# An encoder trunk on one core: recurrence outputs one segment later, weight scales inside the next projection, weight squares and casts in halves

## The chip, the cores and the metric

The kernel runs on one core of one Trainium2 chip. TensorE (PE) multiplies matrices, VectorE (DVE) and ScalarE (ACT) do elementwise work, GpSimd (POOL) does some more of it, and SyncE (SP) issues the DMAs. The metric is the device time of one execution in microseconds; lower is better. Time before: 2451.22 us, the median of 3 runs (2450.67 to 2451.57).

## The reference, cut to what matters

One residual layer of a bidirectional encoder on an input of 2048 positions by 1024 channels. One combined projection of the normalized input makes ten blocks of 1024 columns. Five of them feed a gated linear recurrence with 8 heads and a 128 x 128 state per head, once forward and once backward; three feed a spatial gating branch; two are merge gates. The rest of the layer (two branch projections, one output projection, norms) lies behind what is changed here.

```python
h = _rmsnorm(x, norm_w[layer])
proj = jnp.einsum('bsd,de->bse', h, w_in[layer])
(q_raw, ffwd_raw, fbwd_raw, i_raw, ga_raw, u_raw, v_raw, gb_raw, ma_raw, mb_raw) = jnp.split(proj, split_points, axis=-1)
...
"""S_t = diag(f_t) S_{t-1} + k_t v_t^T ; o_t = S_t^T q_t, chunkwise."""
...
q = heads(jax.nn.silu(q_raw)) * (HGRN_KDIM ** -0.5)
v = heads(i_raw)
k_f, g_f = _hgrn2_forget(ffwd_raw, lb_fwd)
k_b, g_b = _hgrn2_forget(fbwd_raw, lb_bwd)
o_fwd = _gla_chunked(q, heads(k_f), v, heads(g_f))
o_bwd = flip(_gla_chunked(flip(q), flip(heads(k_b)), flip(v), flip(heads(g_b))))
o = (o_fwd + o_bwd).transpose(0, 2, 1, 3)
o = _rmsnorm(o, gnorm_w)
```

## The kernel before

**Number format.** A projection is made of three fp16 matmuls, since both sides are split into a high and a low fp16 part: `mm3` (L207) runs over 8 blocks of the contraction and for each multiplies high by high, high by low and low by high, 24 matmuls in one PSUM bank. The input `xT` is split once. A weight *unit* is 256 columns of `w_in`: `halves` (L171) loads it in fp32 (`wraw`), squares it on ACT to get the sum of squares (L180), casts that sum on GpSimd (`wsb`, L184), sums it over the partitions with a one-column matmul into `misc` (L189), makes a power-of-two scale of it with four small operations on DVE (`pow2`), and then makes the high part on ACT (L199) and the low part on DVE (L200). The first `yield` stands after the square, so `load` (L163) is everything before the `misc` matmul and calling its result is the rest. `unit` (L147) hands out the next unit and keeps up to two more under way. The pool of the units has five buffers of 8 KB a partition, and each unit takes two, so a unit's load waits until an older unit is used up.

**Loops.** `phase1` (L274) goes over four pairs of heads. For each pair it projects the values `i` of all four segments of 512 positions (`v_seg`, 96 matmuls of 256 columns a segment), then for each of the two heads the forward direction over segments 0 to 3 and the backward one over segments 3 to 0. Forward, a segment's query projection (`q_seg`, 24 matmuls of 512 columns) comes before its forget-gate projection (24 more); backward it is the gate projection alone. The first head's queries are projected earlier, beside the input's normalization.

**One segment.** `gla_operands` (L397) projects the gate, takes two sigmoids of it on ACT (`fz` L406, `kk` L408) and makes the decayed operands on DVE with two scans: `ff` (L437, the query side), `kt` (the key side), the decays `e8`, and on GpSimd `q0` (L453), the queries against the state at the segment's begin. `gla_products` (L460) then does, for four blocks of 128 positions: the scores `sc` (L477, L480) and the transposed keys `pk` (L479) on TensorE; the masks on DVE (L485, L498, and backward the sums L507); the copy `ks` of the keys on ACT (L500); the state products `pu` (L513); and then block by block the outputs `po` from scores (L517, backward only, where `at` holds both directions' scores) and from the state before the block (L519), and the state update `st` on DVE (L525). The outputs are evicted on ACT (`of`, L532) or added to the forward ones on DVE (`ob`, L534), squared on ACT (L538), normalized on GpSimd (L539 to L541) and stored in `o_d` (L339).

The work is software-pipelined by one segment: `finish(late)` (L331) runs the products of the segment before, after the operands of the present one. All engines' instructions are put in order when the program is built, by priorities and the builder's own estimate of when things are ready; `high_priority(URGENT)` raises masks, key copies and state updates. Each engine then runs its own list strictly in order and waits on semaphores.

After the recurrence the value projection of the gating branch begins (`wv`, two units of 512 columns each, `values` L761). Six of its tiles are made before a flag is read (L1261) and all engines pass a branch.

Of the kernel before, what the change touches and what calls it, by code (L numbers as in the profile page):

```python
# [27 lines left out]
P = 128  # L28
# [23 lines left out]
class Trunk:  # L52
# [85 lines left out]
    def plan(self):  # L138
# [6 lines left out]
        self.todo, self.made = todo, []  # L145
# [25 lines left out]
    def halves(self, w, c0, width):  # L171
# [3 lines left out]
        for i in range(width):  # L175
# [3 lines left out]
            ss = sm.tile([P, 1], F32, name="wss")  # L179
            nc.scalar.activation(out=(wt[:, 1] if wt is not None else got[0][1][:, 0]), in_=raw, func=AF.Square,  # L180
                                 accum_out=ss)

            sb = sm.tile([P, 1], BF16, name="wsb")
# [4 lines left out]
        for i, (_, _, sb) in enumerate(got):  # L188
            nc.tensor.matmul(pb, self.ones16, sb, start=(i == 0), stop=(i == width - 1))  # L189
# [6 lines left out]
        for raw, wt, _ in got:  # L196
            if wt is None:
                wt = self.wu.tile([P, 2, K, N], F16, name="wsplit")
            nc.scalar.activation(out=wt[:, 0], in_=raw, func=AF.Copy, scale=s)  # L199
# [7 lines left out]
    def mm3(self, ps, lh, ll, rh, rl):  # L207

        nc = self.nc
        for k in range(KT):  # L210
            nc.tensor.matmul(ps, lh(k), rh(k), start=(k == 0), stop=False)  # L211
            nc.tensor.matmul(ps, lh(k), rl(k), start=False, stop=False)  # L212
            nc.tensor.matmul(ps, ll(k), rh(k), start=False, stop=(k == KT - 1))  # L213

# [59 lines left out]
    def phase1(self):  # L274
        nc, tc = self.nc, self.tc
        with ExitStack() as es:
# [7 lines left out]
            self.gs = E(tc.tile_pool(name="g_s", bufs=4, **R))  # L284
# [5 lines left out]
            with tc.tile_pool(name="xp", bufs=3) as self.xp:  # L290
# [8 lines left out]
                for b in range(NSEG):  # L299
# [11 lines left out]
                    qs[b] = self.q_seg(0, 0, b, *wq)  # L311
            self.decays()
# [16 lines left out]
            state, of, late = None, [None] * NSEG, None  # L329

            def finish(seg):  # L331
                nonlocal state
                h, hh, d, s, ops, v = seg
                state, o = self.gla_products(hh, d, *ops, v, state if s != (0 if d == 0 else NSEG - 1) else None,
                                             of[s] if d else None)
                if d == 0:
                    of[s] = o
                else:
                    nc.sync.dma_start(out=self.o_d[4 * s:4 * s + 4, h].rearrange("c p v -> p c v"), in_=o)  # L339

            for hp in range(H // 2):
# [9 lines left out]
                wf = self.unit(self.w_in, C_FF + U * hp)  # L351
                wb = self.unit(self.w_in, C_FB + U * hp)
                for hh in range(2):
                    h = 2 * hp + hh
                    for d in range(2):
                        for s in (range(NSEG) if d == 0 else range(NSEG - 1, -1, -1)):
                            if h and d == 0:
                                qs[s] = self.q_seg(h, hh, s, *wq)
                            ops = self.gla_operands(h, hh, d, s, *(wb if d else wf), qs[s])
# [1074 lines left out]
```

## Time and profile before

| | |
|---|---|
| median of 3 runs | 2451.22 us (2450.67 to 2451.57) |
| the profiled execution's own time | 2447.7 us |
| its span, first to last instruction | 2446.0 us |
| mean granted TensorE clock | 0.995 |
| matmuls in it | 12860 |
| recurrence segments | 8 heads x 2 directions x 4 = 64 |
| their stretch of the span | about 110 to 1016 us |

How to read the rows that follow. A row of the timeline gives the start, the duration, the engine, the line of the kernel, the operation, output and inputs, and how many like it were merged; in brackets stands how long the engine was idle before and who ended that. An fp32 matmul is recorded as two passes, so that "x8" are four of them. A row of the groups by line ends with "busy us, mean ns of one | idle before it and who ended it". A row of the stretches gives the stretch, its length, and busy time (with the number of instructions) of PE, PEld, DVE, ACT and POOL, then the granted clock and the DMA's share and rate. A row of the waits gives the engine, tile and line that waited, for whom, the total, the number and the longest. DMA rows give size and the time from issue to landing.

### The profile page before, as it was taken

The numbers are of one execution on the slowest core, as the hardware profiler recorded it, in microseconds if no ns is written. First come the engines' busy times: TensorE is split into PE (matmuls) and PEld (weight loads), VectorE is DVE, ScalarE is ACT, GpSimd is POOL, SyncE is SP. The second block draws the span as 40 slices with busy tenths as digits, with TensorE's granted clock in tenths as the row PEclk, the third lists the DMA queues.
The fourth block names the chain that finished last, engine by engine and source line by source line (L and its number), as shares of the span: only waits on it lengthen the run. The fifth ranks groups of instructions, "written<-read, shape, count | busy, mean of one in ns | idle before, by whom it ended". The sixth has DMA issues, their size and how long they took to land. (4 is left out here: it accounts for less than half of the span.)

```text
span 2446.0 us, 33707 instructions
## 1 busy us (share of the span) xinstructions
PE 2355.1 (96%) x12860; PEld 1293.8 (53%) x12860; DVE 1523.8 (62%) x3014; ACT 1021.4 (42%) x1811; POOL 320.1 (13%) x523
## 2 busy tenths in 40 slices
PE   7999999999999999999999999999999999999998
PEld 5665766576658565544445544444444444444443
DVE  6686646654765476767555555667765564676754
ACT  6533333333333333423354545666655542244432
POOL 2121202120212021261000000000000000000011
PEclk9999999999999999999999999999999999999999
DMA  5100110011001000202322322577664773777733
GB/s 184 67 10 26 36 35 14 22 36 35 14 23 35 18 14 23 68 29 86 122 94 78 96 90 82 189 267 271 234 232 141 250 267 129 271 245 276 249 122 120
DMA packets 169483, 281.22 MB, mean 115 GB/s; under 512 B 10976, under 2 KB 105184, under 8 KB 162144
## 3 DMA queue, kind: packets, MB, share of 16 engines
q1 hardware_dynamic: 169312, 278.98, 33.6%
q8 instruction: 102, 1.67, 0.3%
q14 instruction: 69, 0.57, 0.1%
HBM read 174.08 MB, written 104.86 MB: 114 GB/s over the span
## 5 line engine op out<-in xcount | busy, mean ns | idle before, releaser
L728 PEld LDWEIGHTS <-seven 128*128 128x128 f16 x5376 | 524.6, 98 | 633.5 <-issue 23.5
L728 PE MATMUL bank<-seven 128*128 128x512 f16 x2016 | 438.2, 379 | 8.5 <-DVE zs L742 7.4
L728 PE MATMUL bank<-xT,seven 128*128 128x512 f16 x1920 | 428.8, 380 | 1.7 <-ACT zs L695 1.6
L728 PE MATMUL bank<-xs,seven 128*128 128x512 f16 x1440 | 322.1, 380 | 0.0
L211 PE MATMUL pin<-xT,wsplit 128*128 128x512 f16 x768 | 291.0, 379 | 0.2 <-ACT xT L256 0.2
L213 PE MATMUL pin<-xT,wsplit 128*128 128x512 f16 x768 | 291.1, 379 | 0.0
L212 PE MATMUL pin<-xT,wsplit 128*128 128x512 f16 x768 | 291.0, 379 | 0.0
L211 PE MATMUL pin<-wsplit,xT 128*128 128x256 f16 (+1 forms) x768 | 239.9, 312 | 11.2 <-ACTq L795 4.7
L213 PE MATMUL pin<-wsplit,xT 128*128 128x256 f16 (+1 forms) x768 | 239.8, 312 | 2.2 <-DVE xT L257 2.1
L212 PE MATMUL pin<-wsplit,xT 128*128 128x256 f16 (+1 forms) x768 | 239.6, 312 | 1.3 <-DVE wsplit L200 1.2
L742 DVE SCALAR_TENSOR_TENSOR zs<-bank,us,zs 128x512 f32<-128x512 f32 x120 | 89.0, 747 | 74.2 <-PE bank L728 71.7
L749 ACT ACTIVATE zs<-zs 128x512 f32<-128x512 f32 x120 | 75.4, 628 | 139.6 <-DVE zs L742 139.3
L742 DVE SCALAR_TENSOR_TENSOR zs<-bank,su,zs 128x512 f32<-128x512 f32 x72 | 53.9, 749 | 108.9 <-PE bank L728 85.4
L410 DVE TENSOR_SCALAR fz<-fz,fb,fa 128x512 f32<-128x512 f32 x64 | 35.7, 558 | 133.1 <-ACT fz L406 133.1
L213 PEld LDWEIGHTS <-wsplit 128*128 128x128 f16 x768 | 75.2, 98 | 79.5 <-issue 3.0
L212 PEld LDWEIGHTS <-wsplit 128*128 128x128 f16 x768 | 75.2, 98 | 71.7 <-issue 1.4
L211 PEld LDWEIGHTS <-wsplit 128*128 128x128 f16 x768 | 77.0, 100 | 67.2
L623 DVE TENSOR_TENSOR tmp<-raw 128x512 f32<-128x512 f32 x64 | 43.9, 690 | 106.6 <-ACT tmp L609 98.7
L519 PE MATMUL po<-st,q 128*128 128x128 f32 x480 | 99.4, 290 | 10.4 <-DVE st L525 7.1
L695 ACT ACTIVATE zs<-bank,us 128x512 f32<-128x512 f32 x120 | 80.6, 678 | 58.7 <-PE bank L728 56.1
L212 PEld LDWEIGHTS <-xT 128*128 128x128 f16 x768 | 76.0, 99 | 44.9 <-issue 10.0
L519 PEld LDWEIGHTS po<-st,q 128*128 128x128 f32 x480 | 72.9, 189 | 48.1 <-DVE st L525 38.6
(202 smaller groups left out, 3610.1 us busy)
## 6 DMA issues: line engine op xcount, KB each, us to landing
kept<-seven SPq DMA_DIRECT2D x16, 1792.0 KB, 7.7
seven<-kept SPq DMA_DIRECT2D x16, 1792.0 KB, 9.6
wraw<-in_w_in_dram SPq DMA_DIRECT2D x20, 1024.0 KB, 5.2
raw<-in_w_in_dram SPq DMA_DIRECT2D x40, 512.0 KB, 4.7
xt<-in_x_dram SPq DMA_DIRECT2D x16, 512.0 KB, 3.9
o_d<-ob SPq DMA_DIRECT2D x32, 256.0 KB, 2.3
v<-V SPq DMA_DIRECT2D x16, 512.0 KB, 3.5
vl<-v SPq DMA_DIRECT2D x32, 256.0 KB, 3.0
```

Of the source, the lines that this page charges most:

```text
L211: nc.tensor.matmul(ps, lh(k), rh(k), start=(k == 0), stop=False)
L212: nc.tensor.matmul(ps, lh(k), rl(k), start=False, stop=False)
L213: nc.tensor.matmul(ps, ll(k), rh(k), start=False, stop=(k == KT - 1))
L410: nc.vector.tensor_scalar(out=f, in0=f, scalar1=fb, scalar2=fa, op0=ALU.mult, op1=ALU.add)
L519: nc.tensor.matmul(po[:, n, :], q0[:, n * P:(n + 1) * P], st, start=(d == 0), stop=True)
L623: sub = lambda out, x, y: self.nc.vector.tensor_tensor(out=out, in0=x, in1=y, op=ALU.subtract)
L695: self.nc.scalar.activation(out=t, in_=ps, func=AF.Copy, scale=su)
L728: nc.tensor.matmul(ps, lhs(x, k), rhs(y, k), start=start and not (k or n), stop=k == 3 and n == 2, skip_group_check=True)
L742: self.nc.vector.scalar_tensor_tensor(out=more, in0=ps, scalar=su, in1=more, op0=ALU.mult, op1=ALU.add)
L749: self.nc.scalar.activation(out=out, in_=more, func=func)
```

## The change

Four edits, all of them in the part before the branch:

- `gla_products` is split in three. `gla_scores` makes scores, masks and key copies, `gla_states` the state products and all four state updates, `gla_outputs` the outputs. `finish` calls the scores, then runs the outputs of the *previous* segment (`flush`), and hangs the state products on a hook. The four states and `q0` of a segment must live longer, so their pool `g_s` gets ten state buffers and three for `q0` and moves to the other side of the memory.
- Hooks: `hook(k, f)` keeps a function that `mm3` calls after contraction block k of the next projection. State products run after block 1, that is after 6 of 24 matmuls, and a unit's scale after block 4.
- The scores' order: transposes and the second half's scores first, the first half's scores later. The masks lose `high_priority`; the key copy keeps it.
- A unit's squares, its two sums and its casts are made in halves of 1024 columns; the scale matmul becomes two one-column matmuls. The gate units are asked for when the first segment that uses them comes.

```diff
 def unit(self, w, c0, ahead=2):
-        self.made = [(k, m() if callable(m) else m) for k, m in self.made]
         while self.todo and len(self.made) < 1 + ahead and not (self.made and len(self.todo[0]) > 2):
-            self.made.append((self.todo[0], self.load(*self.todo.pop(0))()))
+            self.made.append((self.todo[0], self.hook(4, self.load(*self.todo.pop(0)))))
         what, got = self.made.pop(0)
         assert what[0] is w and what[1] == c0
-        return got
+        return got() if callable(got) else got
...
-            ss = sm.tile([P, 1], F32, name="wss")
-            nc.scalar.activation(out=(wt[:, 1] if wt is not None else got[0][1][:, 0]), in_=raw, func=AF.Square,
-                                 accum_out=ss)
+            ss = sm.tile([P, 2], F32, name="wss")
+            junk = wt[:, 1] if wt is not None else got[0][1][:, 0]
+            for h in range(2):
+                ks = slice(h * K // 2, (h + 1) * K // 2)
+                nc.scalar.activation(out=junk[:, ks], in_=raw[:, ks], func=AF.Square, accum_out=ss[:, h:h + 1])
...
-            nc.scalar.activation(out=wt[:, 0], in_=raw, func=AF.Copy, scale=s)
+            for h in range(2):
+                ks = slice(h * K // 2, (h + 1) * K // 2)
+                nc.scalar.activation(out=wt[:, 0, ks], in_=raw[:, ks], func=AF.Copy, scale=s)
...
             nc.tensor.matmul(ps, ll(k), rh(k), start=False, stop=(k == KT - 1))
+            self.run_hooks(k)
+
+    def run_hooks(self, k=KT):
+        todo, self.hooks = [f for n, f in self.hooks if n <= k], [h for h in self.hooks if h[0] > k]
+        for f in todo:
+            f()
...
-            self.gs = E(tc.tile_pool(name="g_s", bufs=4, **R))
...
+            self.gs = E(tc.tile_pool(name="g_s", bufs=10))
             self.decays()
...
             def finish(seg):
-                nonlocal state
+                nonlocal state, outs
                 h, hh, d, s, ops, v = seg
-                state, o = self.gla_products(hh, d, *ops, v, state if s != (0 if d == 0 else NSEG - 1) else None,
-                                             of[s] if d else None)
+                self.run_hooks(2)
+                scores = self.gla_scores(d, *ops[:2], of[s][0] if d else None)
+                flush()
                 if d == 0:
-                    of[s] = o
-                else:
-                    nc.sync.dma_start(out=self.o_d[4 * s:4 * s + 4, h].rearrange("c p v -> p c v"), in_=o)
+                    of[s] = scores[0], self.gof.tile([P, 4, P], F32, name="of")
+                begin = state if s != (0 if d == 0 else NSEG - 1) else None
+
+                def go():
+                    nonlocal state
+                    states = self.gla_states(hh, d, scores[1], ops[3], v, begin)
+                    state = states[-1]
+                    return states
+
+                states = self.hook(1, go)
+
+                def out(at_o=of[s]):
+                    o = self.gla_outputs(hh, d, *at_o, ops[2], v, [begin] + states()[:-1])
+                    if d:
+                        nc.sync.dma_start(out=self.o_d[4 * s:4 * s + 4, h].rearrange("c p v -> p c v"), in_=o)
+
+                outs = out
...
-                wf = self.unit(self.w_in, C_FF + U * hp)
-                wb = self.unit(self.w_in, C_FB + U * hp)
...
+                            if not hh and s == (NSEG - 1 if d else 0):
+                                wfb[d] = self.unit(self.w_in, (C_FB if d else C_FF) + U * hp)
+                            ops = self.gla_operands(h, hh, d, s, *wfb[d], qs[s])
...
-            finish(late)
+                if t == 0:
+                    finish(late)
+            flush()
...
-        for n in range(4):
-            ks = kt[:, n // 2].rearrange("p b c -> p (b c)")
-            if n % 2 == 0:
-                nc.tensor.matmul(s1[:, n:n + 2], ks[:, 0:P], q2[:, n:n + 2, fr], start=True, stop=True)
-            ks = ks[:, P * (n % 2 + 1):P * (n % 2 + 2)]
-            nc.tensor.transpose(pk[:, n, :], ks, self.ident)
-            nc.tensor.matmul(s2[:, n], ks, q2[:, n, lr], start=True, stop=True)
+        for what, n in ((1, 0), (2, 0), (1, 1), (2, 1), (1, 2), (2, 2), (1, 3), (0, 0), (2, 3), (0, 2)):
+            if what == 0:
+                nc.tensor.matmul(s1[:, n:n + 2], keys(n, 0), q2[:, n:n + 2, fr], start=True, stop=True)
+            elif what == 1:
+                nc.tensor.transpose(pk[:, n, :], keys(n, n % 2 + 1), self.ident)
+            else:
+                nc.tensor.matmul(s2[:, n], keys(n, n % 2 + 1), q2[:, n, lr], start=True, stop=True)
...
+    def gla_outputs(self, hh, d, at, o_st, q0, v, states):
+        nc, sm = self.nc, self.sm
+        po = self.pk.tile([P, 4, P], F32, name="po")
+        hs = slice(hh * P, hh * P + P)
+        order = range(4) if d == 0 else range(3, -1, -1)
+        for n, st in zip(order, states):
+            if d:
+                nc.tensor.matmul(po[:, n, :], at[:, n, :], v[:, n, hs], start=True, stop=(st is None))
+            if st is not None:
+                nc.tensor.matmul(po[:, n, :], q0[:, n * P:(n + 1) * P], st, start=(d == 0), stop=True)
```

More of the change, by code (lines that the diff above doesn't have):

```diff
@@ L188, in halves @@
         for i, (_, _, sb) in enumerate(got):
-            nc.tensor.matmul(pb, self.ones16, sb, start=(i == 0), stop=(i == width - 1))
+            for h in range(2):
+                nc.tensor.matmul(pb, self.ones16, sb[:, h:h + 1], start=not (i or h), stop=(i == width - 1 and h == 1))
         s = sm.tile([P, 1], F32, name="ws")
@@ L513, in gla_products @@
             nc.tensor.matmul(pu[:, n, :], ks[:, n, :], v[:, n, hs], start=True, stop=True)
[L514 removed]
+        states = []
         for n in order:
[L516 to L519 removed]
             sn = self.gs.tile([P, P], F32, name="st")
```

77 lines of the change are left out of this document (47 added, 30 removed).

## The prediction, made before the changed kernel ran

> **What bounds the kernel now.** I read the table by stretches for the engine that is full, then TensorE's waits, then TensorE's timeline of one segment of each kind. The change touches only the first part of the program, the projections with the recurrence; the 906 us from 110 to 1016 us hold all 64 recurrence segments (8 heads, 2 directions, 4 segments).
>
> ```profile
> core 0: us, PE busy (x) PEld busy (x) DVE busy (x) ACT busy (x) POOL busy (x), PEclk, DMA share, GB/s
> 110.00:1016.00 906.00, 882.08 (x5649) 580.86 (x5648) 579.10 (x1611) 299.21 (x656) 177.82 (x262) 1.00 0.09 27
> 401.71:412.06 10.35, 10.16 (x66) 6.80 (x64) 8.66 (x25) 3.52 (x12) 4.14 (x6) 1.00 0.10 27
> 382.46:391.64 9.18, 9.01 (x57) 5.88 (x56) 7.28 (x22) 2.46 (x4) 1.37 (x4) 1.00 0.01 2
> ```
>
> TensorE is the bound: busy 882 of 906 us at granted clock 1.00. But the missing 24 us are not all its loss. A matmul of 512 columns counts 0.38 us while the next starts 0.22 us after it, so a stall shorter than that overlap counts as busy. The loss has to be read from starts. The list of TensorE's waits gives the places:
>
> ```profile
> PE po L519 <- DVE st L525: 7.1, 34, 0.5
> PE sc L477 <- DVE ff L437: 5.7, 6, 1.3
> ...
> PE misc L189 <- POOL wsb L184: 2.7, 6, 0.8
> ```
>
> The timeline of a backward segment, from one block of scores to the next:
>
> ```profile
> 401.71 0.38 PE L477 MATMUL sc<-ff,kt 128*128 128x128 f32 x2
> ...
> 403.34 0.38 PE L211 MATMUL pin<-xT,wsplit 128*128 128x512 f16 x1
> ...
> 404.08 1.16 PE L513 MATMUL pu<-vt,ks 128*128 128x128 f32 x8
> 405.07 0.38 PE L211 MATMUL pin<-xT,wsplit 128*128 128x512 f16 x1
> ...
> 405.93 0.39 PE L519 MATMUL po<-st,q 128*128 128x128 f32 x2
> ...
> 406.60 0.39 PE L517 MATMUL po<-vt,at 128*128 128x128 f32 x2
> 407.18 0.49 PE L519 MATMUL po<-st,q 128*128 128x128 f32 x2 [0.19 <-DVE st L525]
> ...
> 408.17 0.38 PE L211 MATMUL pin<-xT,wsplit 128*128 128x512 f16 x1
> ...
> 412.06 0.38 PE L477 MATMUL sc<-ff,kt 128*128 128x128 f32 x2
> ```
>
> The period is 412.06 - 401.71 = 10.35 us. Its content: 18 projection matmuls lie between 408.17 and 412.06, 0.216 us each, so the 24 take 5.19. The scores take 1.63 (401.71 to 403.34), the state products 0.99 (404.08 to 405.07). Three outputs lie between 405.93 and 406.60, 0.223 each, so eight take 1.79. The sum is 9.60; 0.75 us is stall, most of it visible where `po` waits for the state. A forward segment without a query projection:
>
> ```profile
> 382.46 0.38 PE L477 MATMUL sc<-ff,kt 128*128 128x128 f32 x2
> ...
> 384.09 0.44 PE L519 MATMUL po<-st,q 128*128 128x128 f32 x2
> ...
> 384.80 1.13 PE L513 MATMUL pu<-vt,ks 128*128 128x128 f32 x8
> 385.77 0.38 PE L213 MATMUL pin<-xT,wsplit 128*128 128x512 f16 x1
> ...
> 386.75 0.49 PE L519 MATMUL po<-st,q 128*128 128x128 f32 x2 [0.17 <-DVE st L525]
> ...
> 391.64 0.38 PE L477 MATMUL sc<-ff,kt 128*128 128x128 f32 x2
> ```
>
> Period 9.18, content 5.19 + 1.63 + 0.97 + 4 x 0.223 = 8.68, stall 0.50. DVE comes next: busy 8.66 of the 10.35 and 7.28 of the 9.18.
>
> **The change part by part.** *Outputs one segment later* (the `po` matmuls, the `ob`/`of` evictions, the store). In the built program's order TensorE runs, per segment: scores, the previous segment's outputs in one block, 6 projection matmuls, state products, 18 more (42 with a query projection). The states that the outputs read were begun a segment earlier, so the wait of `po` for `st` goes. `ks` (ACT) has the outputs and six matmuls as cover, at least 0.89 + 1.30 = 2.2 us, so the wait before the state products goes too. What is late next would be `ff`, which the next scores need:
>
> ```profile
> 501.84 0.69 ACT L406 ACTIVATE fz<-pin,wus 128x512 f32<-128x512 f32 x1 [1.06 <-PE pin L213]
> ```
> ```profile
> L525 DVE SCALAR_TENSOR_TENSOR st<-st,e,pu 128x128 f32<-128x128 f32 x240 | 80.9, 337 | 0.9
> L507 DVE TENSOR_TENSOR at<-at,ad 64x256 f32<-64x256 f32 x64 | 26.9, 420 | 1.9
> L534 DVE TENSOR_TENSOR ob<-po,of 128x512 f32<-128x512 f32 x32 | 21.8, 682 | 3.0 <-PE po L519 2.4 <-issue 0.7
> ```
>
> The last projection matmul ends 0.38 - 0.22 = 0.16 after the scores' start, the sigmoid takes 0.69, handoffs an estimated 0.1: DVE starts at 0.95. The new order puts three state updates, one mask add and `ob` behind ff·q, 3 x 0.34 + 0.42 + 0.68 = 2.1 us of the backward 8.66, so ff·q ends near 0.95 + 6.56 = 7.5 of a period of 9.6: 2.1 us of cover. Forward, with three updates behind, near 0.95 + 7.28 - 1.0 = 7.2 of 8.68: 1.5 of cover. If that cover went, every microsecond beyond it would be paid on all 64 segments. Saved: 32 x 0.75 + 32 x 0.50 = 40.0 us. From below: nothing, if the stall only moves to `ff` (a rival below). From above: also the slow first pass of a state product after a late `ks`, about 0.1 a segment (0.99 against 8 x 0.111 = 0.89, half an output's 0.223 per pass), 6 us more.
>
> *Scores against a late `ff`.* At the last forward segment of a pair's second head, in three pairs, the present order runs into scores that are not ready:
>
> ```profile
> 240.18 0.38 PE L211 MATMUL pin<-xT,wsplit 128*128 128x512 f16 x1
> 241.66 0.49 PE L477 MATMUL sc<-ff,kt 128*128 128x128 f32 x2 [1.10 <-DVE ff L437]
> ```
>
> 1.48 - 0.22 = 1.26 us, three times: 3.8. The masks lose their urgency, so that DVE's operand chain comes first, and the keys' transposes, which need no `ff`, now lead the block. I take 3.8 as gone, and give back below what a weight's casts still cost there.
>
> *Scale inside the next projection.* All 2.7 us of waits of `misc` should go. A weight lands 5.2 us after its issue and then needs its squares and one cast:
>
> ```profile
> wraw<-in_w_in_dram SPq DMA_DIRECT2D x20, 1024.0 KB, 5.2
> ```
> ```profile
> L199 ACT ACTIVATE wsplit<-wraw,ws 128x2048 f16<-128x2048 f32 x20 | 40.0, 1998 | 8.9 <-DVE ws L135 5.2 <-DVE wus L194 2.1 <-DVE wsplit L200 1.2
> L180 ACT ACTIVATE wsplit<-wraw 128x2048 f16<-128x2048 f32 x20 | 38.2, 1910 | 45.2 <-DMA wraw<-in_w_in_dram 23.0 <-DVE wsplit L200 8.0 <-PE pin L213 7.9
> L180 ACT ACTIVATION_READ_ACCUMULATOR wsplit<-wraw 128x1 f32 x20 | 3.8, 188 | 0.0
> ```
> ```profile
> L200 DVE SCALAR_TENSOR_TENSOR wsplit<-wraw,ws,wsplit 128x2048 f16<-128x2048 f32 x20 | 47.6, 2380 | 29.6 <-ACT wsplit L199 29.6
> ```
>
> That is 5.2 + 1.9 + 0.2 and a small cast, some 7.6 us. The scale matmul of the unit whose buffer the last value projection frees now stands some 32 projection matmuls behind it, 7.0 us; in the new order it stands 52 behind, 11.2. SP's queue keeps its sequence but for one weight load a head pair, which passes two stores of `ob`; it waits for the pair's last projection, and those stores become ready just after. The states' buffers move to where the input tiles lay, which are long free.
>
> *Halves.* Each unit gains one square, one accumulator read (0.19) and one cast. ACT is busy 299 of 906 us, so it hides them everywhere but at the start, where TensorE has no projection to run: about 0.19 + 0.2 + 0.1 = 0.5. The 20 extra scale matmuls are one column wide; bounds 0 and about 0.1 each (a whole 128-column pass is 0.11); I take 0.5 in all.
>
> *What is given back.* (a) One unit in each of these three pairs lands its casts (2.0) and low part (2.38) on that same segment's operands: the sigmoid starts an estimated 1.5 late behind the casts and `ks`, DVE is held by the low part, and `ff` comes some 1.3 late. Four transposes and two outputs that the order pulls ahead cover 4 x 0.11 + 2 x 0.22 = 0.9 of it: 3 x 0.4 = 1.2. (b) The last head prepares the value weights meanwhile, two casts and two low parts, 8.8 us of ACT and DVE in series, and there DVE is the bound now:
>
> ```profile
> 989.47 0.46 PE L517 MATMUL po<-vt,at 128*128 128x128 f32 x2 [0.71 <-DVE at L507]
> ...
> 999.58 0.49 PE L477 MATMUL sc<-ff,kt 128*128 128x128 f32 x2 [1.27 <-DVE ff L437]
> ```
>
> A later output doesn't help that; its four backward segments keep their stall: 4 x 0.75 = 3.0. (c) The scale of the second pair of value weights moves from before the last outputs to behind them. Then 2 x (2.0 + 2.38) and an estimated 0.8 of small steps = 9.6 stand against 36 matmuls x 0.216 = 7.8 us until its last part is read: 1.8, less what is lost there today; 1.5, bounds 0 and 3. (d) Chance collisions on DVE, 0.5.
>
> Sum: 40.0 + 3.8 + 2.7 - 0.5 - 0.5 - 1.2 - 3.0 - 1.5 - 0.5 = 39.3 us. The profiled execution took 2447.7 us (span 2446.0) and would take 2408.4. The median of the runs is 2451.2, 3.5 above it, so the forecast is **2412 us**.
>
> **Rivals.** *A ring between DVE and ACT.* In the new order `ob` stands behind ff·q on DVE, and on ACT the four squares of `ob` stand ahead of the next segment's sigmoid:
>
> ```profile
> 509.70 0.31 ACT L538 ACTIVATE osq<-ob 128x128 f32<-128x128 f32 x1 [4.70 <-DVE ob L534]
> ...
> 510.79 0.19 ACT L538 ACTIVATION_READ_ACCUMULATOR osq<-ob 128x1 f32 x1
> ```
>
> The squares take 510.98 - 509.70 = 1.28. If this closes in every tight backward period (three a head, 24), the period is 8.66 less one state update (0.34) plus 1.28 + 0.69 + 0.1 = 10.4 in place of 9.6: 24 x 0.8 = 19 us lost, **2431**. For it: it is longer than 9.6. Against: only one of a head's four `ob` stands ahead of a sigmoid in the tight run; two fall into periods with a query projection, about 5 us longer.
>
> *The ring with GpSimd in DVE's way: slower.* A scan that took 2.00 started beside a GpSimd product:
>
> ```profile
> 999.78 2.00 DVE L421 TENSOR_TENSOR_SCAN w<-fz,wd 128x512 f32<-128x512 f32 x1
> ```
> ```profile
> 999.67 1.04 POOL L453 TENSOR_TENSOR q<-ff,e 128x512 f32<-128x512 f32 x1 [1.22 <-DVE fs L413]
> ```
> ```profile
> L421 DVE TENSOR_TENSOR_SCAN w<-fz,wd 128x512 f32<-128x512 f32 x32 | 39.6, 1237 | 0.2
> ```
>
> The mean is 1.24. If both large GpSimd products of a segment (`q0`, `ob`) block DVE for their whole 1.04, the ring is 12.5 us, and 24 x 2.9 = 70 us are lost: **2482**. It ends above today from a ring of 9.6 + 39.3 / 24 = 11.2 us on. Against: the mean of 1.24 over 32 scans leaves room for hardly more than that one collision. The Trainium skill, SBUF — State Buffer, section "SBUF: two separate sides", says that the two engines share one pair of ports as an exclusive lock and that the later one blocks for the whole instruction; the 2.00 us scan agrees, and by that rule every overlap would cost up to the 1.04 above.
>
> *It does not do what it says:* the stall moves whole from the state to `ff`. The waits list already has `ff` second, but for six events only. Then nothing changes, **2451**. *Better:* the first passes and all that is given back vanish too, 6 + 6 us more: **2400**.
>
> **How the numbers follow.** Forecast 0.70 (its own range 2400 to 2426), ring 0.13, better 0.09, stall moves 0.04, slower ring 0.04. The range of 8 in 10 runs from 2398 to 2433: it takes in the better case and the ring. A change under 0.2% (5 us) can't be told from none here. Faster: 0.70 + 0.13 + 0.09 = 0.92; within 0.2%: 0.04; slower: 0.04.
>
> **What would show it.** Right: backward periods of 9.6 and forward of 8.7, `po` for `st` and `misc` for `wsb` gone from the waits, scores that seldom wait for `ff` before the last head, about 1.5 us of TensorE waits at the second value weights. Wrong: tight backward periods of 10.4 with ACT's sigmoid behind the squares (ring), DVE operations far over their means (GpSimd), or waits of `sc` for `ff` in every segment.

## The result, and the profile after

The changed kernel took 2434.22 us, the median of 4 runs (2431.60 to 2437.65), against 2451.39 for the kernel before in the same session: a ratio of 0.9932, 95% interval 0.9916 to 0.9948. It is faster by 17 us, less than half of the 39 us forecast, and just outside the forecast's range. The profiled execution took 2434.28 us. Its page:

```profile
span 2432.5 us, 33850 instructions
...
PE 2334.8 (96%) x12880; PEld 1299.2 (53%) x12880; DVE 1535.1 (63%) x3014; ACT 1020.4 (42%) x1871; POOL 315.9 (13%) x523
```

The view by stretches, for the same forward and the same tight backward segment that the prediction showed:

```profile
core 0: us, PE busy (x) PEld busy (x) DVE busy (x) ACT busy (x) POOL busy (x), PEclk, DMA share, GB/s
...
374.72:383.32 8.60, 8.60 (x57) 5.88 (x56) 7.41 (x22) 2.35 (x4) 1.24 (x3) 1.00 0.00 0
391.92:401.19 9.27, 9.27 (x63) 6.55 (x62) 8.96 (x26) 2.13 (x4) 1.46 (x3) 1.00 0.01 2
```

TensorE is now busy without a gap: 8.60 us a segment in place of 9.18, and 9.27 in place of 10.35 (this backward segment carries the outputs of the direction's first segment, which has one output matmul fewer; full ones come to 9.50, the 14.68 us of a period with a query projection less its 24 x 0.216). DVE is busy 8.96 of the 9.27, so little is left before it would be the bound. The steady segments reach the lengths that were forecast. The list of TensorE's waits shows what came besides. The first line is from the profile before, the others from the one after:

```profile
PE pu L513 <- ACT ks L500: 1.3, 4, 0.5
```
```profile
PE pu L568 <- ACT ks L546: 10.1, 3, 3.4
...
PE sc L529 <- DVE ff L486: 3.1, 3, 1.0
...
PE misc L191 <- POOL wsb L185: 2.4, 6, 0.9
```

`po` for `st` is gone. But the state products now wait three times for the key copy `ks`, 3.4 us each, once at the start of each later pair of heads. Before the change `pu` waited for `ks` 1.3 us in all. The waits of `misc` for `wsb` are hardly shorter (2.7 us before), and `sc` still waits for `ff` three times.

To add it up, I took each TensorE matmul's start minus the start of the one before it, less the distance that undisturbed matmuls of its kind keep (0.216 us for 512 columns, 0.109 for 256, 0.112 for an fp32 pass of 128, 0.085 for one of 64). What is left is called *excess* from here on. The stretch up to the conditional block (the branch on the flag) falls into five groups: the start with the first segment, 53 steady segments, the three segments where `sc` waited for `ff`, the three at a pair's start, and the last head with the first value tiles. Behind the branch and the value tiles, from the first `bank` matmul to the last matmul, the traces of before and after hold the same TensorE instructions in the same order; I call it the late stretch.

| us | before | after | difference |
|---|---|---|---|
| start and first segment, excess | 19.3 | 17.8 | -1.5 |
| 53 steady segments, excess | 40.3 | 3.8 | -36.5 |
| three segments with `sc` late for `ff`, excess | 7.1 | 4.6 | -2.5 |
| three segments at a pair's start, excess | 3.9 | 17.2 | **+13.3** |
| last head up to the block, excess | 8.0 | 9.9 | +1.9 |
| late stretch, length | 1249.6 | 1261.2 | **+11.6** |

The sum is -13.7; the spans differ by 13.5. So in this pair of profiles two places took back 25 us.

**A pair's start.** ACT's timeline of the changed kernel at the second pair:

```profile
272.07 0.31 ACT L604 ACTIVATE osq<-ob 128x128 f32<-128x128 f32 x1 [4.42 <-DVE p2t L130]
...
273.25 2.17 ACT L203 ACTIVATE wsplit<-wraw,ws 128x1024 f16<-128x1024 f32 x2
275.45 0.69 ACT L430 ACTIVATE vt<-pin,wus 128x512 f32<-128x512 f32 x1
278.07 1.06 ACT L182 ACTIVATE wsplit<-wraw 128x1024 f16<-128x1024 f32 x1 [1.94 <-DVE wsplit L204]
...
279.13 1.04 ACT L182 ACTIVATE wsplit<-wraw 128x1024 f16<-128x1024 f32 x1
...
280.17 0.67 ACT L430 ACTIVATE vt<-pin,wus 128x512 f32<-128x512 f32 x1
280.74 0.30 ACT L604 ACTIVATE osq<-ob 128x128 f32<-128x128 f32 x1
...
281.03 0.58 ACT L546 ACTIVATE ks<-pk 128x512 f32<-128x512 f32 x1
```

And TensorE there (the last of the previous segment's outputs, the scores, projections of 256 columns, then the state products):

```profile
275.61 0.39 PE L593 MATMUL po<-st,q 128*128 128x128 f32 x2
275.83 0.27 PE L527 MATMUL pk<-ident,kt 128*128 128x128 f32 x1
...
277.20 0.44 PE L525 MATMUL sc<-ff,kt 128*128 128x128 f32 x2
277.47 0.27 PE L215 MATMUL pin<-wsplit,xT 128*128 128x256 f16 x1
...
281.66 2.07 PE L568 MATMUL pu<-vt,ks 128*128 128x128 f32 x8 [3.37 <-ACT ks L546]
```

The scores end at 277.6, but in ACT's queue `ks` stands behind the casts of one weight unit, a value eviction, the squares of the *next* unit, another eviction and one square of `ob`. The squares in turn wait until DVE has read the first unit's raw weights for its low part, since that frees their buffer. DVE's timeline shows why all this is late:

```profile
271.30 0.68 DVE L600 TENSOR_TENSOR ob<-po,of 128x512 f32<-128x512 f32 x1
271.90 0.14 DVE L130 TENSOR_SCALAR p2t<-misc 128x1 f32<-128x1 f32 x1
...
272.45 0.16 DVE L135 RECIPROCAL ws<-winv 128x1 f32<-128x1 f32 x1
...
275.46 2.58 DVE L204 SCALAR_TENSOR_TENSOR wsplit<-wraw,ws,wsplit 128x2048 f16<-128x2048 f32 x1 [2.79 <-ACT wsplit L203]
```

The unit's scale starts at 271.90 behind the operands, states and `ob` of the last backward segments, though its `misc` matmul ran at 265.15. From there a chain runs across both engines: scale, casts, low part, squares, `ks`. The kernel before had the same chain:

```profile
281.39 2.00 ACT L199 ACTIVATE wsplit<-wraw,ws 128x2048 f16<-128x2048 f32 x1 [0.97 <-DVE ws L135]
...
285.81 1.91 ACT L180 ACTIVATE wsplit<-wraw 128x2048 f16<-128x2048 f32 x1 [1.71 <-DVE wsplit L200]
...
288.48 0.60 ACT L500 ACTIVATE ks<-pk 128x512 f32<-128x512 f32 x1
```

And its TensorE:

```profile
288.28 0.33 PE L480 MATMUL sc<-ff,kt 128*128 128x64 f32 x2
...
289.13 1.16 PE L513 MATMUL pu<-vt,ks 128*128 128x128 f32 x8
```

From the casts to `ks` it took 7.1 us before and 7.8 after, hardly a difference. What changed is TensorE: its last score matmul now begins 3.95 us after the casts (277.20 - 273.25), before it was 6.89 (288.28 - 281.39). Its scores reach the place 11 us earlier than before the change, the casts 8 us earlier: TensorE has gained 3 us on a chain that hasn't become faster.

**The clock adds to it.** The stall itself is 3 x 3.5 = 10.5 us of the 17.2. Another 4.9 us come from matmuls at half clock right behind it, 3.1, 0.1 and 1.8 after the three stalls (rows of two separate looks by stretches, right after the first and the second of these stalls):

```profile
281.66:285.66 4.00, 4.00 (x18) 3.32 (x19) 1.39 (x4) 1.20 (x7) 2.24 (x3) 0.50 0.00 0
...
517.80:521.80 4.00, 3.64 (x33) 3.36 (x34) 1.39 (x4) 1.56 (x8) 2.24 (x3) 1.00 0.00 0
```

After the first stall the granted clock was 0.50 and the matmuls took twice their time for some 6 us; after the second, as long a stall, it stayed at 1.00. So one 3.5 us stall cost between 3.6 and 6.6 us here; the last section shows what decides it.

**The late stretch** of before, and then of after:

```profile
1186.48:2436.06 1249.58, 1218.22 (x5825) 572.75 (x5824) 768.61 (x1129) 596.29 (x970) 54.91 (x135) 1.00 0.54 185
```
```profile
1161.45:2422.65 1261.20, 1221.78 (x5825) 574.26 (x5824) 768.78 (x1129) 595.76 (x970) 54.22 (x135) 0.99 0.53 183
```

The counts are the same on every engine, the length isn't. Whether that is chance was the first question for the experiments.

### The profile page after: what moved, and what is told of

Same layout as the page of the kernel before. It is cut to its first block, busy times and chain, and to the rows that moved or that the text cites. A ratio compares the mean times of both kernels' runs of the same rounds, so it can differ in the third digit from the quotient of the medians.

```text
span 2432.5 us, 33850 instructions
## 1 busy us (share of the span) xinstructions
PE 2334.8 (96%) x12880; PEld 1299.2 (53%) x12880; DVE 1535.1 (63%) x3014; ACT 1020.4 (42%) x1871; POOL 315.9 (13%) x523
## 5 line engine op out<-in xcount | busy, mean ns | idle before, releaser
L502 POOL TENSOR_TENSOR q<-ff,e 128x512 f32<-128x512 f32 x64 | 73.6, 1150 | 371.7 <-DVE e L500 231.0
L455 ACT ACTIVATE fz<-pin,wus 128x512 f32<-128x512 f32 x64 | 43.9, 686 | 143.1 <-PE pin L217 142.9
L216 PEld LDWEIGHTS <-xT 128*128 128x128 f16 x768 | 76.5, 100 | 44.7 <-issue 9.7
L217 PEld LDWEIGHTS <-xT 128*128 128x128 f16 x768 | 76.4, 99 | 44.2 <-DVE xT L280 5.0
```

The source lines that it names most:

```text
L455: nc.scalar.activation(out=fz[:, 1:SEG + 1], in_=ps, func=AF.Sigmoid, scale=us)
L502: nc.gpsimd.tensor_tensor(out=q0.rearrange("p (m c) -> p m c", c=64), in0=ff.rearrange("p (m c) -> p m c", c=64), in1=e8.rearrange("p n b ...
```

## The experiments

Each kernel was timed beside the kernel before on the same chip. The medians of before were 2447.1 us beside after_again, before_again, fix_boundary and no_halves; 2445.3 beside fix_all_units, outputs_at_once, scale_at_unit and scores_old_order; 2448.2 beside the other four. So the ratios are the figures to compare.

| kernel | us | ratio (95%) | steady | `sc` for `ff` | pair's start | last head | late stretch |
|---|---|---|---|---|---|---|---|
| before, first profile | 2451.4 | 1 | 40.3 | 7.1 | 3.9 | 8.0 | 1249.6 |
| after, first profile | 2434.2 | 0.9932 (0.9916-0.9948) | 3.8 | 4.6 | 17.2 | 9.9 | 1261.2 |
| after_again | 2429.1 | 0.9918 (0.9905-0.9932) | 3.7 | 4.6 | 16.8 | 9.9 | 1257.9 |
| before_again | 2447.4 | 1.0004 (0.9995-1.0014) | 40.2 | 6.9 | 3.7 | 8.0 | 1254.5 |
| before_third | one run, 2444.0 | - | 40.2 | 6.8 | 3.8 | 8.0 | 1249.7 |
| fix_boundary | 2412.1 | **0.9862** (0.9847-0.9877) | 3.7 | 4.5 | 1.7 | 10.5 | 1253.8 |
| fix_all_units | 2410.1 | **0.9851** (0.9834-0.9867) | 2.5 | 0.1 | 1.8 | 8.8 | 1258.6 |
| no_halves | 2427.8 | 0.9922 (0.9908-0.9935) | 4.7 | 4.4 | 16.9 | 9.4 | 1255.6 |
| scale_at_unit | 2430.1 | 0.9938 (0.9921-0.9954) | 3.7 | 4.5 | 15.8 | 11.1 | 1255.2 |
| scores_old_order | 2427.4 | 0.9928 (0.9911-0.9944) | 17.1 | 3.9 | 4.7 | 8.9 | 1256.9 |
| outputs_later_only | 2427.1 | 0.9914 (0.9897-0.9931) | 16.9 | 4.3 | 3.3 | 8.6 | 1257.8 |
| fix_scores_old | 2426.9 | 0.9907 (0.9888-0.9926) | 17.0 | 3.9 | 2.1 | 7.2 | 1254.7 |
| before_unit_later | 2446.6 | 0.9989 (0.9979-0.9999) | 41.3 | 6.8 | 3.8 | 8.0 | 1252.4 |
| outputs_at_once | 2528.0 | 1.0343 (1.0326-1.0360) | 115.8 | 6.9 | 3.6 | - | 1254.8 |

Columns four to seven are excess in us as in the table above, each from one profile, the last column is a length; one group of outputs_at_once isn't given, and the start isn't shown, since it moved by up to 5 us between executions without a pattern.

**after_again, before_again and before_third**: nothing edited.

> The changed kernel once more, nothing edited. In its first profile the stretch from the first bank matmul to the end, whose instructions and addresses are the same as before the change, took 1261.2 us against 1249.6. Theory (chance): that stretch varies by several us from execution to execution, so a second profile lands anywhere between 1249 and 1262, while the first part repeats: the conditional block ends at 1018 within 1 us and each of the three `ks` waits at 3.5. Rival (the change slows the later part, by a denser first part that leaves a lower granted clock): 1261 again within 1.5 us.

> The kernel before once more, nothing edited. Theory (chance): its stretch from the first bank matmul to the end is not tied to 1249.6 us but lies between 1249 and 1262. Rival (the change slows the later part): 1249.6 again within 1.5 us. The ratio also shows what the measurement tells from no change.

> One more profile of the kernel before. Its stretch from the first bank matmul to the end took 1249.6 and 1254.5 us in two profiles; eight profiles of kernels with the change lie between 1253.8 and 1261.2 with the same instructions. Theory (chance): anywhere between 1249 and 1259. Rival (before has the shorter stretch): under 1252.

The first part repeats: the conditional block ended at 1016.9 us (1018.0 in the first profile), the three `ks` waits were 3.49 to 3.51, and every group agrees within half a microsecond. The late stretch doesn't: 1257.9 after 1261.2, and for the kernel before 1254.5 and 1249.7 after 1249.6. So some 6 or 7 of the 11.6 us are the chance of the first pair of profiles. Not all: the four profiles of the kernel before and of before_unit_later (1249.6, 1254.5, 1249.7, 1252.4) average 1251.6, the ten of the changed kernel and its variants 1256.7. All three new profiles lie in the wide ranges that chance was given, but that didn't settle it: before_third lies under the 1252 of its rival too. A denser first part is an unlikely reason: outputs_at_once has the slowest first part of all and still 1254.8. In the stretch many waits of 1 to 2 us come and go from run to run, and the difference builds up at no single place. Why it is some 5 us on average stays open.

**fix_boundary**: the next unit is taken up behind the scores.

```diff
-                    wi = self.unit(self.w_in, C_I + U * hp)
+                    wi = self.unit(self.w_in, C_I + U * hp, ahead=1)
...
                             finish(late)
                             late = None
+                            self.top_up()
...
+    def top_up(self, n=2):
+        while self.todo and len(self.made) < n and not (self.made and len(self.todo[0]) > 2):
+            self.made.append((self.todo[0], self.hook(4, self.load(*self.todo.pop(0)))))
```

> At a head pair's start the next weight unit is taken up only behind the scores of the last backward segment, so that in ACT's queue `ks` stands ahead of that unit's casts and of the squares that wait for its low part. Theory (`ks` late behind casts and squares): the three waits of the state products for `ks` (3.5 us each) go, the excess of the three boundary segments falls from 17.2 us to under 4, and the time from 2434 to about 2421. First rival (`ks` is late for the value evictions and the squares of `ob` that stand ahead of it, not for the weight): the waits stay over 2 us, 2430 or more. Second rival (the unit now comes late): new waits of `misc` or of projections for the low part, 3 us or more, and less than half of the 13 us is gained.

2412.1 us, 17 less than after_again, where 13 were expected; the excess at the pairs' starts falls by 15. Its ACT timeline at the same place:

```profile
275.44 0.31 ACT L609 ACTIVATE osq<-ob 128x128 f32<-128x128 f32 x1 [1.94 <-DVE ob L605]
275.75 0.58 ACT L551 ACTIVATE ks<-pk 128x512 f32<-128x512 f32 x1
...
280.09 2.19 ACT L207 ACTIVATE wsplit<-wraw,ws 128x1024 f16<-128x1024 f32 x2 [2.34 <-DVE ws L135]
...
284.69 1.06 ACT L186 ACTIVATE wsplit<-wraw 128x1024 f16<-128x1024 f32 x1 [1.58 <-DVE wsplit L208]
```

`ks` now runs ahead of casts and squares, and TensorE goes straight on to the state products:

```profile
275.76 0.44 PE L530 MATMUL sc<-ff,kt 128*128 128x128 f32 x2
...
276.69 1.06 PE L573 MATMUL pu<-vt,ks 128*128 128x128 f32 x8
```

The wait is gone from the list and the three segments' excess falls from 17 to 1.7. Two evictions and a square of `ob` still stand ahead of `ks`, and do no harm: the first rival is out. So is the second: the waits of `misc` are 2.2 us in all, no more than with the change. The theory holds.

**before_unit_later**: the same edit in the kernel before.

> The kernel before, with the next unit taken up behind the scores at a pair's start as in the mended version. Theory (before the change `ks` is just in time there, and only the change uncovers it): the three segments' excess goes from 3.7 us to 2 to 3.5, the time is within 3 us of before. Rival (the mend is a gain of its own): 8 us or more under before.

Within 3 us (0.9989), and the pair's start unchanged at 3.8. The edit isn't a gain of its own; it takes away something that only the change uncovers.

**scores_old_order** and **fix_scores_old**: the old loop over the scores, and the masks urgent again, in the changed kernel and in fix_boundary.

```diff
-        for what, n in ((1, 0), (2, 0), (1, 1), (2, 1), (1, 2), (2, 2), (1, 3), (0, 0), (2, 3), (0, 2)):
+        for n in range(4):
...
         with self.tc.high_priority(URGENT):
+            if d == 0:
+                first_half(at[fr, :, fr])
...
             nc.scalar.activation(out=ks, in_=pk, func=AF.Copy)
-        if d == 0:
-            first_half(at[fr, :, fr])
```

> The changed kernel with the scores' matmuls in the old order and the masks urgent again; outputs later, halves and scale stay. Forecast's term (3.8 saved against a late `ff`, 1.2 given back): the three segments in which `sc` waits for `ff` go from 4.5 to about 7 us, time 2 to 3 us over the changed kernel. Rival (the urgent masks put the operand chain back on every segment): steady excess rises by more than 10 us. Other rival (the order does nothing): within 1 us everywhere.

> The version that takes up the next unit behind the scores at a pair's start, with the old order of the scores and urgent masks. Theory (what the new order saves on `ff` in the steady segments is paid back whole at the boundary unless the boundary is mended): now the old order costs its full 13 us: steady excess 17 instead of 3.7, the time about 2424, 12 to 14 us over that version. Rival (the order of the scores is worth nothing by itself): within 2 us of that version.

The time of the changed kernel doesn't move (0.9928), but everything under it does. TensorE's waits in scores_old_order:

```profile
PE sc L525 <- DVE ff L486: 10.6, 12, 1.4
...
PE pu L567 <- ACT ks L549: 2.2, 3, 0.7
```

The scores now wait for `ff` in nine more segments: steady excess is 13.4 us larger, and the pair's start 12 us smaller. ACT's chain there takes as long (7.86 us from the casts to `ks`, 7.78 in the changed kernel), only TensorE arrives later, held up upstream. DVE's rows show where, in a segment whose scores began at 388.57 us:

```profile
391.13 1.04 DVE L533 TENSOR_TENSOR ad<-sc,mask 64x128 f32<-64x128 f32 x3
392.20 0.85 DVE L556 TENSOR_TENSOR at<-at,ad 64x256 f32<-64x256 f32 x2
392.98 1.21 DVE L470 TENSOR_TENSOR_SCAN w<-fz,wd 128x512 f32<-128x512 f32 x1
```

The urgent masks run ahead of the first scan, which starts 4.4 us behind the scores; in the changed kernel's like segment it started 2.4 us behind them. So the masks' priority is likely the greater part. The order of the scores and the priority weren't run apart. In fix_boundary, where nothing is left to pay at the pair's start, the old order costs what it saves elsewhere:

```profile
PE sc L530 <- DVE ff L491: 10.7, 12, 1.4
```

0.9907 against 0.9862, steady 17.0 against 3.7. The new order with its lower priority is worth 13 us by excess (11 by the ratios), and the changed kernel paid nearly all of it back at the three pair starts. My second expectation said so; of the first, its first rival was nearest, though it didn't foresee that the pair's start would pay for it.

**outputs_later_only**: squares, casts and scale, scores' order and masks as before; outputs later, state products on the hook and the gate units at their first use stay.

> The changed kernel with halves, scale inside the projection, the scores' order and the masks' priority all put back; outputs one segment later and state products inside the projection stay. Theory (the later outputs carry the gain; the other edits only move stall to the pair boundary): as the run with the old order of the scores, steady excess about 17 us, boundary about 5, the conditional block ended at 1016 within 2 us, 17 to 20 us under before. Rival (the other edits carry part of it): less than 14 us under before.

0.9914, steady 16.9, pair's start 3.3, the conditional block ended at 1013.8 us, 21 us under before in its session: a microsecond or two better than the theory has it, by a start that was shorter in this execution. The later outputs, with the state products on the hook and the gate units at their first use, bring the whole of the changed kernel's gain; these three weren't run apart. The other edits together bring nothing, of which one, the scores' order with the masks' priority, brings 13 and loses them again.

**no_halves**: one square, one sum and one cast a unit.

```diff
-            for h in range(2):
-                ks = slice(h * K // 2, (h + 1) * K // 2)
-                nc.scalar.activation(out=wt[:, 0, ks], in_=raw[:, ks], func=AF.Copy, scale=s)
+            nc.scalar.activation(out=wt[:, 0], in_=raw, func=AF.Copy, scale=s)
```

> Squares and casts of weights in one instruction each, as before the change; all else as changed. Theory (`ks` is late because of the queue's order, the halves only lengthen the queue): each of the three `ks` waits falls from 3.5 to about 3 us, and the time by 1 to 3 us, to 2431 to 2433. Rival (the halves alone make `ks` late): the waits fall under 0.5 us and the time to about 2421. Other rival (the halves help): slower by 2 us or more, at the start above all.

0.9922 lies between the changed kernel's two measurements. The three `ks` waits fell from 3.5 to 3.34 us, not to 3. The halves are worth nothing that can be measured either way.

**scale_at_unit**: the unit's scale where the unit is asked for.

```diff
-            self.made.append((self.todo[0], self.hook(4, self.load(*self.todo.pop(0)))))
+            self.made.append((self.todo[0], self.load(*self.todo.pop(0))()))
```

> The changed kernel with each weight's scale worked out where its unit is taken up, as before the change, not after the fifth step of the next projection. Forecast's term (2.7 us of `misc` waits gone): 2 to 3 us slower than the changed kernel, with `misc` waits longer. Theory after the first trace (the waits of `misc` are set by squares that wait for a buffer, 2.4 us left with the change): within 1.5 us of the changed kernel. Rival (the scale so placed comes later on DVE and makes the casts late at the boundary): the three `ks` waits fall by 2 us or more each, 8 us or more faster.

0.9938, with the intervals of the two other measurements overlapping; `misc` waits 2.4 us as with the change, `ks` 10.0. So there is no sign of the 2.7 us, and none of the rival.

**outputs_at_once**: `flush()` right behind `outs = out`.

> The changed kernel with each segment's outputs put right behind its own scores and states again; halves, scale inside the projection and the new order of the scores stay. Theory (the gain is the wait of the outputs for the state): the excess of the 53 steady segments goes from 3.7 us back to about 40, as before the change. Then the boundary tells who made `ks` late: if the later outputs did, its three segments fall from 17 us to about 4 and the time is 2 to 5 us under before; if the other parts did, they stay near 17 and the time is 8 to 13 us over before. Rival (the steady gain came from the other parts): steady excess stays under 10 us, time still 10 us or more under before.

Neither. It came out 83 us slower than before, with steady excess of 116 us:

```profile
PE po L592 <- DVE at L558: 34.8, 18, 2.9
```

Asked for at once, the outputs pull the state products with them, and both stand right behind the scores with no projection between. The kernel before had projections there. So this isn't the old arrangement, and it says nothing on who made `ks` late; outputs_later_only took its place. What it does show is how much the distance between scores and outputs is worth.

**fix_all_units**: beside fix_boundary, the unit that was cast in the last forward segments is taken up in the value projections too.

```diff
-                                wfb[d] = self.unit(self.w_in, (C_FB if d else C_FF) + U * hp)
+                                wfb[d] = self.unit(self.w_in, (C_FB if d else C_FF) + U * hp, ahead=1 if d else 2)
...
-                    wi = self.unit(self.w_in, C_I + U * hp)
+                    wi = self.unit(self.w_in, C_I + U * hp, ahead=0)
...
+                        self.top_up(min(NSEG - b, 2))
```

> As the version that takes up the next unit behind the scores at a pair's start, and beside it the unit that is now cast during the last forward segments is taken up there too, one value projection later. Theory (casts and low part in a tight segment are what delays `ff` and `ks`): beside the `ks` waits, the three waits of `sc` for `ff` (1.2 us each) and the 0.3 us waits of `misc` two segments earlier go too: another 4 to 5 us under that version, about 1.5% under before in all. Rival (two units' casts in the value projections collide there): new waits of `misc`, of the value projections or of the first operands eat it up, no faster than that version.

The waits of `sc` for `ff` are gone from the list, their segments' excess falls from 4.5 to 0.1, and three of the six waits of `misc` go:

```profile
PE misc L728 <- POOL wsb L683: 3.2, 2, 2.1
...
PE misc L195 <- POOL wsb L189: 1.7, 3, 0.7
```

(The first of these rows is in the late stretch.) The conditional block ends at 996.1 us against 1001.4, as expected. The late stretch of this profile took 4.8 us more and hides most of that in the span; the medians, 2410.1 and 2412.1 in different sessions, don't tell the two versions apart. Both beat the changed kernel and the one before.

## Why the prediction was wrong, by its own steps

**Outputs one segment later, -40.0.** The mechanism was right, and the steady segments came out as computed: forward 8.60 (8.7 said), full backward ones 9.50 (9.6), no stall of `po` for `st` left, and no ring between DVE and ACT. The attribution was wrong. Of the 36.5 us gained there the later outputs bring 23.4 (40.3 to 16.9), and the scores' order with the masks' lower priority, added to them, the other 13. The text booked the whole gain under the outputs. It also had too much cover for `ff`: 2.1 us backward and 1.5 forward. In the changed kernel's tight segments `ff` was ready 0.7 to 1.0 us and 1.05 us ahead of the scores; here is the end of the backward segment shown above, whose next scores begin at 401.19:

```profile
399.81 0.68 DVE L486 TENSOR_TENSOR ff<-ff,q 128x512 f32<-128x512 f32 x1
```

So it held, with less to spare than was thought.

**"`ks` (ACT) has the outputs and six matmuls as cover ... so the wait before the state products goes too."** This is the step that failed. It was worked out for a steady segment and carried to all. At a pair's start neither half of it holds: the value loop runs the outputs ahead of the scores, so they cover nothing; the six matmuls have 256 columns there, 0.65 us in place of 1.30; and ACT's queue holds casts and squares of weights ahead of `ks`. Measured: 17.2 us of excess in place of 3.9, 10.5 of it stall and 4.9 half clock behind it; with fix_boundary 1.7. Its list of what is given back named the casts for the last forward segment and the last head, not for this place. Of the same kind is the assumption under all terms that the distance between ACT's weight chain and TensorE stays as it was. TensorE came to the second pair's start 11 us earlier, the chain, which hangs on DVE, only 8.

**Scores against a late `ff`, -3.8, and (a), +1.2.** Together -2.6, and those three segments did lose 2.5 us of excess, but that agreement is luck. By the starts of the matmuls the wait for `ff` went only from 1.26 to 1.20 us in each, 0.2 in all. The rest is the wait of `po` for `st` in the same segments, 0.68 us each before and none after, which the sum had under the outputs already. The order's main effect, 13 us in other segments, wasn't in the sum.

**Scale inside the projection, -2.7.** Mis-sized: 2.4 of the 2.7 us of `misc` waits remain, at the same two places of a pair (0.35 and 0.87 us by the matmuls' starts at the first pair, now 0.32 and 0.67). The text took 7.6 us from the load to the scale. The changed kernel's ACT shows what was left out, for a load issued at 318.39:

```profile
327.03 1.06 ACT L182 ACTIVATE wsplit<-wraw 128x1024 f16<-128x1024 f32 x1 [1.84 <-DVE wsplit L204]
```

The squares write into a buffer that another unit's low part still reads, and the `misc` matmul came at 330.14, 11.75 us after the issue.

**Halves at the start, +0.5, extra matmuls, +0.5, chance collisions, +0.5.** Too small to be seen; no_halves shows no difference.

**(b) and (c), the last head.** In the sum the four backward segments gain and lose 3.0, and (c) adds 1.5; measured +1.9. Right in total, and (c) by itself: the wait for the second value weights' low parts is 2.0 us by the matmuls' starts, 0.3 before.

**Left out of the sum: the late stretch.** It was taken as unchanged, and its TensorE instructions are. The first pair of profiles differs by 11.6 us there, all profiles by 5 on average. A range that counts on a stretch of 1250 us not to move by 0.4% is too narrow.

Of the 26 us between the forecast's 39.3 and the 13.7 of the first pair of profiles, 13 are the pair's start and 12 the late stretch. With the pair's start mended the kernel is 35 us under before in its session (2447.1 to 2412.1), against 39 forecast. The 4 us that are left are of the size of the late stretch's share (2.2 us over the mean of before in this profile, 5 over all).

**The rivals.** None of them came. DVE and ACT closed no ring; its price was too high as well, since only two backward periods of a head hold no query projection (10.07 and 10.35 us before), not three. GpSimd didn't hold DVE up by more than a few collisions, the scan's mean having gone from 1237 to 1303 ns:

```profile
L470 DVE TENSOR_TENSOR_SCAN w<-fz,wd 128x512 f32<-128x512 f32 x32 | 41.7, 1303 | 0.8
```

The stall's move to `ff` was nearer than its 0.04: without the new order and the masks' lower priority 13 of the 36.5 us go there.

## What to carry to other kernels

A stall removed in a tight loop can move the bound engine earlier in time against chains that other engines run at their own pace; look for the next place in the program where the two meet, not only at the loop's steady state. For each copy that stands on the critical path, list what its engine's queue holds ahead of it at the loop's seams as well, weight preparation above all, and put that work where the bound engine has long runs of its own. And when an edit measures as nothing, look whether one part of the program gained what another lost: here the scores' order measured as nothing, and with the second place mended it was worth 11 to 13 us.

## What the runs showed of the hardware

The cost of a TensorE stall isn't its length. Over thirteen of the profiles (all but outputs_at_once, from 100 us on) I counted stalls and looked whether six or more matmuls in the 7 us after them kept twice their distance:

| stall, us | stalls | followed by half clock | extra time then, mean |
|---|---|---|---|
| 1.2 to 1.6 | 143 | 0 | - |
| 1.6 to 2.0 | 55 | 3 | 1.6 |
| 2.0 to 2.4 | 28 | 10 | 1.5 |
| 2.4 to 3.3 | 23 | 17 | 1.5 |
| over 3.3 | 50 | 44 | 1.7 |

So in these runs a stall under 1.6 us costs its length, and one over 2.4 us mostly 1.5 us more. What decides is where the stall falls. The granted clock in these traces changes only on a grid of 3.41 us. I laid TensorE's work (each matmul at its undisturbed distance) over that grid, in all fourteen profiles from 110 us on, and took the steps of the grid that ran at full clock:

| TensorE at work, share of a step | steps | next step at half clock |
|---|---|---|
| under 0.36 | 85 | 85 |
| 0.38 to 0.395 | 9 | 7 |
| 0.40 and over | 9290 | 0 |

The three stalls of the changed kernel show it. The first left 0.16 of a step for work, the third 0.07, and half clock followed. The second lay across two steps with 0.43 and 0.48 of work, and the clock stayed. A step at half clock does half a step's work, so it takes at most 3.41 / 2 = 1.7 us, near the 1.5 to 1.7 of the table; after the first stall there were two such steps, since the stall reached 0.7 us into the first of them, which held 0.39 of work. So what counts is how much idle time falls into one step: some 2.1 us of it, 0.61 x 3.41, in one stall or several. The Trainium skill, TensorE: Matmul & The Clock Gate, section "Why this matters for your kernels", advises against idle gaps of more than about 3 us and says that one window of idle time brings the clock back to half; its section "Part 1: The HAM clock gate (the "warmup" mystery)" has a free-running window of 3413 ns. The grid of 3.41 us agrees with that window, and that a 3.5 us stall sometimes passed at full clock and a 1.9 us one sometimes didn't agrees with a rule that looks at where a stall lies. But the gaps that already cost something were shorter here than the 3 us of that rule: a step with up to 0.39 of work in it was enough.
